# First stage of a hybrid diffusion step: roots of the token norms by pairs of tiles with a GpSimd power, and another order of weight loads and steps

## The chip, the cores and the metric

The kernel runs on one core of one Trainium2 chip. The metric is the device time of one execution in microseconds (us); the time before is the median of three runs. One further execution was taken with the hardware profiler, and every row and start time below is from it. The engines are called as in the profile: PE is TensorE (PEld its weight loads), DVE is VectorE, ACT is ScalarE, POOL is GpSimd, SP is SyncE, which here only issues DMAs.

## The reference, cut to what matters

One layer of a diffusion backbone works on 128 context tokens and 512 latent tokens, five tiles of 128 tokens, with 1024 channels, all in float32. The stage that is changed is the very first one:

```python
def rms_scale(x):
    xf = x.astype(jnp.float32)
    return xf * lax.rsqrt(jnp.mean(xf * xf, axis=-1, keepdims=True) + EPS)

def adaln(cond, w_mod, b_mod):
    m = jax.nn.silu(cond) @ w_mod + b_mod
    return jnp.split(m[..., None, :], 6, axis=-1)
...
        sh1, sc1, g1, sh2, sc2, g2 = adaln(c_ctx, w_mod[l], b_mod[l])
        h = rmsnorm(xp, norm1_g[l]) * (1.0 + sc1) + sh1
        y, (k_c, v_c, sf_c, sb_c) = token_mixer(h, *mix_w, pos_ctx, None)
```

`token_mixer` begins with `z = h @ w_in`. The kernel computes the columns of `z` for keys and values first, and those products end the stage. Attention, retention, the output projections and the gated MLP follow; none of their source is changed.

## The kernel before, in words

**Tiling.** The five token tiles lie in `xin`, tokens on the partitions. Each tile's sum of squares is taken on ACT (`x_square`, L340, with an accumulator that is read out after each tile), the reciprocal root on DVE (`rsqrt`, L202 to L220: an integer first guess and three Newton steps), and each tile is scaled in place on DVE (L349). PE transposes a scaled tile in eight 128x128 blocks, four to a PSUM bank (`x_trans`, L356), and the banks are copied out (L358) into `xnT`, two tiles `f0.s.1` and `f0.s.2` that hold channel blocks 0 to 3 and 4 to 7 with the channels on the partitions. PSUM has five banks for this (`mm1.mm`) and three more (`aux1.aux`).

**adaLN.** The product of the two condition vectors with the first 2048 columns of `w_mod` is cut into five groups (`MG`): groups 0 and 1 of one channel block each, groups 2, 3 and 4 of two. For group g, `mod_load(g)` loads the weights, `mod_mm(g)` is the product on PE (L368), `mod_row(g)` copies its result on DVE (L376), and `mod_vec(g)` turns the row into per-channel factors with one small matmul (L382) and two small DVE operations (L384, L386).

**Keys and values.** For each channel block k, `mod_hi(k)` applies the factors to `xnT` on DVE (L391, two instructions) and rounds the result into `hT[0]` on ACT (L393); `mod_lo(k)` forms the rest that rounding left in `hT[1]` on DVE (L396). The weights are split likewise, two channel blocks at a time: `kv_hi(k)` on ACT (L319), `kv_lo(k)` on DVE (L324). `z_kv(k)` then runs 15 matmuls of 128x512 on PE, three for each of five token tiles (`mm3`, L159 to L161): high times high, high activations times low weights (this one waits for `kv_lo`), low activations times high weights (this one waits for `mod_lo`). The five banks accumulate over k from 0 to 7. `z_kv(k, g)` with a second argument places `mod_vec(g)` behind its second token tile, so that PE still has nine matmuls after the small one.

**What sets the order.** Inside the block that begins at L406 the order of PE, DVE and ACT is the written one (`manual_schedule`). After the block, DVE and ACT go back to the scheduler, which also mixes in early work of the next stage. DMAs are issued by SP in the order in which they are written from L327 on; each waits for buffers, and for earlier DMAs on its semaphore. The weight buffers `raw` number two and the split ones (`wh`) eight, so the loads of the next stage wait until these splits are done. The next stage starts with the query columns (`a_group`, L175), whose first matmuls follow the last of `z_kv(7)` on PE. Of POOL the first stage makes no use: its first arithmetic is at L525, for the rotary tables. A similar power of -0.5 on POOL, with one Newton step behind it on DVE, stands at the end of the kernel (`root`, L1250 to L1258).

Of the kernel before, what the change touches and what calls it, by code (L numbers as in the profile page):

```python
# [69 lines left out]
def hybrid_step(ctx: ExitStack, tc: tile.TileContext, a: dict, o: dict):  # L70
# [265 lines left out]
    nc.sync.dma_start(cst[:, C_RF:], a["cst"][:, C_RF:])

# [2 lines left out]
        nc.scalar.activation(sq, xin[:, t, :], AF.Square, accum_out=ss[:, t:t + 1])  # L340

    def x_scale(t0, t1_, on_act=()):
        rs = rsqrt(t1, ss[:, t0:t1_], t1_ - t0, 1.0 / DM)
        for t in range(t0, t1_):
            r = rs[:, t - t0:t - t0 + 1]
            if t in on_act:
                nc.scalar.activation(xin[:, t, :], xin[:, t, :], AF.Copy, scale=r)
            else:
                V.tensor_scalar(xin[:, t, :], xin[:, t, :], r, None, op0=ALU.mult)  # L349

    def x_trans(t):
        for g in range(2):
            ps = mm([P, 512], tag="mm")
            for j in range(4):
                k = g * 4 + j
                nc.tensor.transpose(ps[:, j * P:(j + 1) * P], xin[:, t, k * P:(k + 1) * P], ident)  # L356
# [1 line left out]
            copy(xnT[g][:, :, t * P:(t + 1) * P], ps.rearrange("p (k t) -> p k t", k=4))  # L358
# [1180 lines left out]
```

## Time and profile before

| what | value |
| --- | --- |
| median of three runs | 1196.1 us (1194.02 to 1198.86) |
| the profiled execution: its own time | 1197.29 us |
| the profiled execution: its span, first to last instruction | 1195.5 us |
| instructions | 18334 |
| 0 to 15.5 us: PE busy, DVE busy, ACT busy | 0.37, 4.01, 7.25 us |
| 27.15 to 38.0 us: PE busy, mean granted clock | 10.85 us, 0.84 |
| 38.0 to 49.9 us: PE busy, mean granted clock | 11.77 us, 1.00 |
| 49.9 to 64.0 us: PE busy, mean granted clock | 14.10 us, 1.00 |
| 120 to 1107 us: PE busy | 983.5 of 987 us |

How to read it: the span is one microsecond or two shorter than the time, which includes what lies around the instructions. The rows by stretch of time are from the view of windows. PE's busy time counts each matmul to its modelled end, so that a PE that is shown busy can still have short waits between matmuls. The last `z_kv` matmul starts at 63.83 us, and the first of the query columns at 64.06 us.

### The profile page before, as it was taken

Reading aid. Unit: us, or ns where it says so; the run is one execution under the profiler, and the core shown is the slowest. Engines: PE = TensorE matmul, PEld = TensorE weight load, DVE = VectorE, ACT = ScalarE, POOL = GpSimd, SP = SyncE. Lnnn points to the kernel's source line nnn. Section 1 sums busy time; section 2 is a strip of 40 time slices with the busy share of each in tenths; the row PEclk is TensorE's granted clock in tenths of the full one; section 3 lists DMA queues with packets and bytes.
Section 4 is the critical chain, followed back from the end, with each engine's and each line's share of the span. In section 5 each row is a group of like instructions: output and inputs, shape, how many; then the busy total and the mean of one; then the engine's idle time right before and its main releaser. Section 6 shows DMA issues by size and latency. Waiting matters only on the chain. (4 is left out here: it accounts for less than half of the span.)

```text
span 1195.5 us, 18334 instructions
## 1 busy us (share of the span) xinstructions
PE 1155.4 (97%) x7317; PEld 1040.5 (87%) x7317; DVE 735.7 (62%) x1429; ACT 569.3 (48%) x1022; POOL 173.5 (15%) x176
## 2 busy tenths in 40 slices
PE   3999999999999999999999999999999999999994
PEld 3788899999988888888999988999999899899884
...
GB/s 283 280 108 71 36 36 36 36 57 166 201 210 154 141 98 44 36 36 71 36 77 89 169 124 183 76 106 124 130 126 174 153 91 147 125 134 168 122 140 88
DMA packets 131205, 140.07 MB, mean 117 GB/s; under 512 B 26272, under 2 KB 98032, under 8 KB 131120
## 3 DMA queue, kind: packets, MB, share of 16 engines
...
q14 instruction: 28, 0.23, 0.1%
...
## 5 line engine op out<-in xcount | busy, mean ns | idle before, releaser
L791 POOL TENSOR_TENSOR ret.r2k.6_3635<-ret.u5.5_3528,ret.u1.1_3521 128x256 f32<-128x256 f32 x2 | 1.4, 740 | 205.1 <-ACT ret.u5.5_3528 L787 205.1
L1353 DVE TENSOR_TENSOR t7.u4.4_6930<-t7.u4.4_6930,const.u1.1_70 128x322 f32<-128x322 f32 x10 | 4.9, 494 | 10.1 <-ACT const.u1.1_70 L1352 10.1
L840 DVE SCALAR_TENSOR_TENSOR ret2.u1.1_4322<-ret2.u1.1_4322,const.u14.14_94 64x128 f32<-64x128 f32 x24 | 6.8, 336 | 6.6 <-ACT ret2.u1.1_4322 L833 6.5
L525 POOL TENSOR_TENSOR p1.u1.1_618<-p1.u3.3_622,p1q.u1.1_612 128x512 f32<-128x512 f32 x1 | 1.6, 1567 | 58.6 <-DMA p1.u4.4_624<-in_cache_k 58.6
L152 DVE TENSOR_TENSOR weights.wh.183_6570<-weights.raw.181_6567,weights.wh.182_6569 128x1024 fp32r<-128x1024 f32 x1 | 1.2, 1224 | 14.3 <-ACT weights.wh.182_6569 L147 14.3
L356 PE MATMUL mm1.mm.1_180<-const.u1.1_70,xin.u1.1_112 128*128 128x128 f32 x4 | 1.1, 434 | 9.2 <-DVE xin.u1.1_112 L349 9.2
L1264 POOL TENSOR_TENSOR x1.u1.1_6381<-x1.u1.1_6381,weights.raw.410_10994 128x512 f32<-128x512 f32 x5 | 7.4, 1499 | 16.0 <-ACT x1.tm.112_11007 L1242 9.8
L842 DVE SCALAR_TENSOR_TENSOR ret2.u1.1_4322<-ret2.u1.1_4322,const.u14.14_94 64x128 f32<-64x128 f32 x24 | 6.6, 382 | 4.8 <-ACT ret2.u1.1_4322 L835 4.8
L793 DVE TENSOR_TENSOR ret.u5.5_3528<-ret.u5.5_3528,ret.u1.1_3521 128x512 f32<-128x512 f32 x5 | 3.5, 692 | 9.4 <-POOL ret.r2k.8_3706 L791 3.3
L393 ACT CAST acts.u1.1_100<-f0.s.1_113 128x640 fp32r<-128x640 f32 x4 | 2.9, 727 | 12.9 <-DVE f0.s.1_113 L391 12.9
L793 DVE TENSOR_TENSOR ret.u4.4_3527<-ret.u4.4_3527,ret.u1.1_3521 128x512 f32<-128x512 f32 x5 | 3.5, 692 | 9.0 <-POOL ret.r2k.11_3886 L791 4.7
L356 PEld LDWEIGHTS mm1.mm.1_180<-const.u1.1_70,xin.u1.1_112 128*128 128x128 f32 x4 | 0.7, 216 | 9.4 <-DVE xin.u1.1_112 L349 9.4
L393 ACT CAST acts.u1.1_100<-f0.s.2_114 128x640 fp32r<-128x640 f32 x4 | 2.9, 730 | 9.9 <-DVE f0.s.2_114 L391 9.9
L152 DVE TENSOR_TENSOR weights.wh.108_4352<-weights.raw.106_4349,weights.wh.107_4351 128x1024 fp32r<-128x1024 f32 x1 | 1.2, 1224 | 10.3 <-ACT weights.wh.107_4351 L147 10.3
L147 ACT CAST weights.wh.112_4507<-weights.raw.111_4505 128x1024 fp32r<-128x1024 f32 x1 | 1.0, 1049 | 13.3 <-PE mm3.mm.36_4220 L160 13.3
L902 POOL TENSOR_TENSOR f0.s.5_3525<-f0.s.5_3525,ret2.ny20.11_4904 128x512 f32<-128x512 f32 x5 | 6.0, 1236 | 9.1 <-DVE ret2.ny20.11_4904 L219 9.1
L494 ACT ACTIVATE f0.s.3_724<-f0.s.3_724,p1q.ny20.11_892 128x128 f32<-128x128 f32 x20 | 6.0, 388 | 2.5 <-DVE p1q.ny20.11_892 L217 2.5
...
L259 DVE COPY mod2.wr.9_4312<-aux3.aux.15_4279 128x128 f32<-128x128 f32 x1 | 0.3, 291 | 10.9 <-PE aux3.aux.15_4279 L256 10.9
L1236 DVE TENSOR_TENSOR x1.u1.1_6381<-x1.u1.1_6381,gate.u1.1_5311 128x512 f32<-128x512 f32 x10 | 6.9, 686 | 0.0
L147 ACT CAST weights.wh.67_3361<-weights.raw.66_3359 128x1024 fp32r<-128x1024 f32 x1 | 1.0, 1044 | 11.5 <-PE mm3.mm.8_3143 L195 11.5
L147 ACT CAST weights.wh.72_3539<-weights.raw.71_3537 128x1024 fp32r<-128x1024 f32 x1 | 1.0, 1044 | 11.5 <-PE mm3.mm.12_3298 L195 11.5
...
## 6 DMA issues: line engine op xcount, KB each, us to landing
...
xin.u1.1_112<-in_x_sample SPq DMA_DIRECT2D x4, 512.0 KB
p0.u5.5_130<-in_w_mod SPq DMA_DIRECT2D x2, 1024.0 KB
p0.u6.6_135<-in_w_mod SPq DMA_DIRECT2D x2, 1024.0 KB
p0.u7.7_138<-in_w_mod SPq DMA_DIRECT2D x2, 1024.0 KB
...
```

What stands on the lines that cost most here:

```text
L147: nc.scalar.copy(hi, rv)
L152: (lo_eng or V).tensor_sub(lo, rv, hi.bitcast(F32))
L356: nc.tensor.transpose(ps[:, j * P:(j + 1) * P], xin[:, t, k * P:(k + 1) * P], ident)
L393: nc.scalar.copy(hT[0][:, k, :], xk)
L494: nc.scalar.activation(x[:, j], x[:, j], AF.Copy, scale=rstd[:, j:j + 1])
L793: V.tensor_mul(z, z, r1[:, t, 0:1, :].to_broadcast([P, 8, 64]))
L840: V.scalar_tensor_tensor(Ss[0:64, hh, st + 1, j], Ss[0:64, hh, st, j], cdsel[0:64, h:h + 1], Ss[0:64, hh, st + 1, j], op0=ALU.mult, op1=AL ...
L842: V.scalar_tensor_tensor(Ss[64:128, hh, 2 - st, j], Ss[64:128, hh, 3 - st, j], cdsel[64:128, h:h + 1], Ss[64:128, hh, 2 - st, j], op0=ALU. ...
L902: nc.gpsimd.tensor_mul(ov, ov, rso[:, 4 * t:4 * t + 4].unsqueeze(2).to_broadcast([P, 4, P]))
L1236: V.tensor_mul(x1[:, t, gs], x1[:, t, gs], gb[:, t == 0, gs])
L1264: eng.tensor_mul(x, x, fg[:, c0:c0 + 512])
L1353: V.tensor_sub(u[1][:, hi_u], u[1][:, hi_u], u3[i])
```

## The change

The roots of the token norms are no longer taken for three tiles and then two, but for tiles 0 and 1, then 2 and 3, then 4. The integer first guess and two of the three Newton steps are gone; a power of -0.5 on POOL (`x_sum`) and one Newton step on DVE (`x_root`) stand in their place. `x_scale`, `x_trans` and the copy out of PSUM (`x_evac`) are separate calls now, so that they can be put in any order, and the first adaLN product `mod_mm(0)` stands between the transposes of tiles 2 and 3. The constant -0.5 for the power moves in the constants' table, so that it comes with the first of its two loads. In the DMA order `mod_load(2)` goes ahead of `kv_load(2, 2)`, and `mod_load(3)` ahead of `kv_load(4, 4)`. Behind `z_kv(0)` the steps stand in another order: `kv_hi(2)` and `kv_lo(2)`, which were ahead of `mod_mm(2)`, come after `mod_hi(2)`; `kv_hi(4)` and `kv_lo(4)` come after `mod_hi(4)`; and `mod_mm(4)` stands behind `z_kv(4)`, not ahead of it, so that `mod_vec(4)` is inside `z_kv(5)`.

```diff
-C_ID, C_SEL, C_SEL1, C_JV, C_RF, C_RB, C_MF, C_MB, C_IQ, C_NH, C_W = 0, 128, 136, 140, 142, 270, 398, 526, 654, 786, 787
+C_ID, C_SEL, C_SEL1, C_JV, C_NH, C_RF, C_RB, C_MF, C_MB, C_IQ, C_W = 0, 128, 136, 140, 142, 143, 271, 399, 527, 655, 787
...
     mod_load(1)
+    mod_load(2)
     kv_load(2, 2)
-    mod_load(2)
+    mod_load(3)
     kv_load(4, 4)
-    mod_load(3)
     mod_load(4)
...
-    def x_scale(t0, t1_, on_act=()):
-        rs = rsqrt(t1, ss[:, t0:t1_], t1_ - t0, 1.0 / DM)
...
+    def x_sum(t0, n):
+        m, mh, y = (t1([P, n], tag=f"{g}{t0}") for g in ("xm", "xh", "xy"))
+        V.tensor_scalar(m, ss[:, t0:t0 + n], 1.0 / DM, EPS, op0=ALU.mult, op1=ALU.add)
+        nc.gpsimd.tensor_tensor(y, m, cst[:, C_NH:C_NH + 1].to_broadcast([P, n]), op=ALU.pow)
+        V.tensor_scalar(mh, m, -0.5, None, op0=ALU.mult)
+        xr[t0] = mh, y
+
+    def x_root(t0, n):
+        mh, y = xr[t0]
+        tt = t1([P, n], tag=f"xt{t0}")
+        if n == 1:
+            V.scalar_tensor_tensor(tt, y, mh, y, op0=ALU.mult, op1=ALU.mult)
+        else:
+            V.tensor_mul(tt, y, y)
+            V.tensor_mul(tt, tt, mh)
+        V.scalar_tensor_tensor(y, tt, 1.5, y, op0=ALU.add, op1=ALU.mult)
...
-        x_scale(0, 3)
+        x_sum(0, 2)
+        x_root(0, 2)
+        x_scale(0)
         x_trans(0)
+        x_scale(1)
         x_trans(1)
+        x_sum(2, 2)
+        x_evac(0, 0, A)
+        x_evac(0, 1, A)
+        x_root(2, 2)
+        x_scale(2)
+        x_sum(4, 1)
+        x_evac(1, 0, A)
+        x_trans(2)
+        x_scale(3)
+        x_root(4, 1)
+        x_scale(4)
+        x_evac(1, 1, A)
+        mod_mm(0, False)
+        x_evac(2, 0, A)
+        x_trans(3)
+        x_evac(2, 1, D)
+        mod_row(0)
+        x_evac(3, 0, A)
+        x_evac(3, 1, D)
+        x_trans(4)
+        mod_vec(0)
+        x_evac(4, 0, A)
+        x_evac(4, 1, D)
         kv_hi(0)
-        x_scale(3, 5)
-        x_trans(2)
-        x_trans(3)
-        x_trans(4)
-        mod_mm(0)
-        mod_vec(0)
...
         z_kv(0)
-        kv_hi(2)
-        kv_lo(2)
         mod_mm(2)
         z_kv(1, 2)
         mod_hi(2)
+        kv_hi(2)
+        mod_lo(2)
+        kv_lo(2)
         mod_hi(3)
-        mod_lo(2)
         mod_lo(3)
         z_kv(2)
-        kv_hi(4)
-        kv_lo(4)
         mod_mm(3)
         z_kv(3, 3)
         mod_hi(4)
+        kv_hi(4)
+        mod_lo(4)
+        kv_lo(4)
         mod_hi(5)
-        mod_lo(4)
         mod_lo(5)
         kv_hi(6)
         kv_lo(6)
+        z_kv(4)
         mod_mm(4)
-        z_kv(4, 4)
+        z_kv(5, 4)
         mod_hi(6)
+        mod_lo(6)
         mod_hi(7)
-        mod_lo(6)
         mod_lo(7)
-        z_kv(5)
```

Three places show how the instructions stand now. The first is the start of the stage on DVE. Before, the root of three tiles (`ssx` holds the sums of squares) begins so:

```order
L207 TENSOR_SCALAR p0.nm3.10_160<-p0.ssx.2_115 128x3
L208 TENSOR_SCALAR p0.ni3.11_161<-p0.nm3.10_160 128x3
L209 TENSOR_SCALAR p0.ny3.12_162<-p0.ni3.11_161 128x3
L210 TENSOR_SCALAR p0.nm3.10_160<-p0.nm3.10_160 128x3
L215 TENSOR_TENSOR p0.nt3.13_163<-p0.ny3.12_162 128x3
L216 TENSOR_TENSOR p0.nt3.13_163<-p0.nt3.13_163,p0.nm3.10_160 128x3
L217 SCALAR_TENSOR_TENSOR p0.ny3.12_162<-p0.nt3.13_163,p0.ny3.12_162 128x3
```

The last three of these, one Newton step, follow twice more, and then L349 scales tiles 0, 1 and 2.

Of the change, on the same engine and at the same place (`xy0` and `xy2` come from POOL, which has one instruction of L347 for each pair):

```order
L346 TENSOR_SCALAR p0.xm0.10_160<-p0.ssx.2_115 128x2
L348 TENSOR_SCALAR p0.xh0.11_161<-p0.xm0.10_160 128x2
L357 TENSOR_TENSOR p0.xt0.13_166<-p0.xy0.12_162 128x2
L358 TENSOR_TENSOR p0.xt0.13_166<-p0.xt0.13_166,p0.xh0.11_161 128x2
L359 SCALAR_TENSOR_TENSOR p0.xy0.12_162<-p0.xt0.13_166,p0.xy0.12_162 128x2
L364 TENSOR_SCALAR xin.u1.1_112<-xin.u1.1_112,p0.xy0.12_162 128x1024 x2
```

Thirteen small operations before the first scale have become five, and they wait for two tiles' sums, not three; between L348 and L357 DVE waits for POOL.

The second place is ACT from the first channel block to `kv_hi(6)`. Before, with `weights.wh.5`, `wh.7` and `wh.9` the high parts of the key and value weights from k = 2, 4 and 6 on (the first row is blocks 0 and 1, the third blocks 2 and 3, the fifth blocks 4 and 5):

```order
L393 CAST acts.u1.1_100<-f0.s.1_113 128x640 x2
L319 CAST weights.wh.5_338<-weights.raw.1_124 128x1024
L393 CAST acts.u1.1_100<-f0.s.1_113 128x640 x2
L319 CAST weights.wh.7_419<-weights.raw.2_133 128x1024
L393 CAST acts.u1.1_100<-f0.s.2_114 128x640 x2
L319 CAST weights.wh.9_485<-weights.raw.2_133 128x1024
```

And in the changed kernel, where the cast of `mod_hi` is at L411:

```order
L411 CAST acts.u1.1_100<-f0.s.1_113 128x640 x3
L319 CAST weights.wh.5_390<-weights.raw.1_124 128x1024
L411 CAST acts.u1.1_100<-f0.s.1_113 128x640
L411 CAST acts.u1.1_100<-f0.s.2_114 128x640
L319 CAST weights.wh.7_471<-weights.raw.2_136 128x1024
L411 CAST acts.u1.1_100<-f0.s.2_114 128x640
L319 CAST weights.wh.9_480<-weights.raw.2_136 128x1024
```

The weight split for k = 2 stood ahead of the cast of block 2 and stands behind it now, and the one for k = 4 stands behind the cast of block 4.

The third place is DVE in the same stretch of the changed kernel, from the row of group 2 to block 3. Here L394 to L404 are `mod_row` and `mod_vec`, L409 and L414 are `mod_hi` and `mod_lo`, and L324 is `kv_lo(2)`, which stood ahead of all of these before:

```order
L394 COPY p0.mrow.24_366<-aux1.aux.6_333 128x128
L402 TENSOR_TENSOR p0.u1.1_111<-aux1.aux.7_374,const.u3.3_83 128x2x4
L404 TENSOR_TENSOR p0.u1.1_111<-p0.u1.1_111,const.u3.3_83 128x4
L409 TENSOR_SCALAR f0.s.1_113<-f0.s.1_113,p0.u1.1_111 128x512
L409 TENSOR_SCALAR f0.s.1_113<-f0.s.1_113,p0.u1.1_111 128x128
L414 TENSOR_TENSOR acts.u2.2_101<-f0.s.1_113,acts.u1.1_100 128x640
L324 TENSOR_TENSOR weights.wh.6_391<-weights.raw.1_124,weights.wh.5_390 128x1024
```

Block 3's own L409 and L414 follow behind this L324, where before both blocks' L391 came one after the other.

More of the change, by code (lines that the diff above doesn't have):

```diff
@@ L340, in x_square, with x_scale, x_evac @@
         nc.scalar.activation(sq, xin[:, t, :], AF.Square, accum_out=ss[:, t:t + 1])
-    def x_scale(t0, t1_, on_act=()):
-        rs = rsqrt(t1, ss[:, t0:t1_], t1_ - t0, 1.0 / DM)
[L344 to L349, printed above, removed]
+    xr = {}
+    def x_sum(t0, n):
[13 more added lines that the diff above has]
+        V.scalar_tensor_tensor(y, tt, 1.5, y, op0=ALU.add, op1=ALU.mult)
+        for t in range(t0, t0 + n):
+            xr[t] = mh, y, y[:, t - t0:t - t0 + 1]
+    def x_scale(t):
+        V.tensor_scalar(xin[:, t, :], xin[:, t, :], xr[t][2], None, op0=ALU.mult)
+    xps = {}
     def x_trans(t):
         for g in range(2):
-            ps = mm([P, 512], tag="mm")
+            xps[t, g] = mm([P, 512], tag="mm")
             for j in range(4):
                 k = g * 4 + j
-                nc.tensor.transpose(ps[:, j * P:(j + 1) * P], xin[:, t, k * P:(k + 1) * P], ident)
-            copy = V.tensor_copy if g and t > 1 else nc.scalar.copy
-            copy(xnT[g][:, :, t * P:(t + 1) * P], ps.rearrange("p (k t) -> p k t", k=4))
+                nc.tensor.transpose(xps[t, g][:, j * P:(j + 1) * P], xin[:, t, k * P:(k + 1) * P], ident)
+    def x_evac(t, g, copy):
+        copy(xnT[g][:, :, t * P:(t + 1) * P], xps[t, g].rearrange("p (k t) -> p k t", k=4))
     mrow, psm = {}, {}
@@ L416, in hybrid_step @@
         V.tensor_copy(s128[:, :, 0:2], s32)
+        A, D = nc.scalar.copy, V.tensor_copy
         for t in range(NT):
             x_square(t)
-        x_scale(0, 3)
+        x_sum(0, 2)
+        x_root(0, 2)
+        x_scale(0)
         x_trans(0)
+        x_scale(1)
         x_trans(1)
-        kv_hi(0)
-        x_scale(3, 5)
-        x_trans(2)
-        x_trans(3)
-        x_trans(4)
-        mod_mm(0)
-        mod_vec(0)
+        x_sum(2, 2)
[21 more added lines that the diff above has]
+        x_evac(4, 1, D)
+        kv_hi(0)
         mod_mm(1, False)
@@ L435, in hybrid_step @@
         mod_hi(1)
+        mod_lo(1)
         kv_lo(0, 1)
-        mod_lo(1)
         kvb = [mm([P, 512], tag="mm") for _ in range(NT)]
         z_kv(0)
-        kv_hi(2)
-        kv_lo(2)
         mod_mm(2)
```

## The prediction

> **What bounds the kernel now.** I read the page first, then the waits of PE, then the timeline of the first 65 us, then windows around the places where PE pauses.
>
> ```profile
> PE 1155.4 (97%) x7317; PEld 1040.5 (87%) x7317; DVE 735.7 (62%) x1429; ACT 569.3 (48%) x1022; POOL 173.5 (15%) x176
> PE mm1.mm.1_180 L356 <- DVE xin.u1.1_112 L349: 9.2, 1, 9.2
> 14.69 2.08 DVE L349 TENSOR_SCALAR xin.u1.1_112<-xin.u1.1_112,p0.ny3.12_162 128x1024 f32<-128x1024 f32 x3
> 15.50 1.11 PE L356 MATMUL mm1.mm.1_180<-const.u1.1_70,xin.u1.1_112 128*128 128x128 f32 x4 [9.15 <-DVE xin.u1.1_112 L349]
> 27.18 0.48 PE L159 MATMUL mm1.mm.11_318<-weights.wh.3_204,acts.u1.1_100 128*128 128x512 f32 x1
> ```
>
> PE is busy for 97% of the span, and its only long waits are in the first stage: 9.2 us for the first scaled tile, then the way to the first `z_kv` matmul at 27.18. From there to the query columns it hardly stops. So a gain here is a gain of the whole only if PE reaches the end of `z_kv(7)` sooner, and each new pause of PE behind 27.18 takes from it at full price.
>
> **The roots.** Before, the first scale waits for three sums and thirteen small operations.
>
> ```profile
> 10.82 0.19 ACT L340 ACTIVATION_READ_ACCUMULATOR acts.u2.2_101<-xin.u1.1_112 128x1 f32 x1
> 12.32 0.17 DVE L207 TENSOR_SCALAR p0.nm3.10_160<-p0.ssx.2_115 128x3 f32<-128x3 f32 x1 [4.82 <-ACT acts.u2.2_101 L340]
> 1174.78 0.17 DVE L1249 TENSOR_SCALAR t7.rm.28_11067<-t7.rm.28_11067 128x3 f32<-128x3 f32 x1
> 1175.95 0.17 DVE L1251 TENSOR_SCALAR t7.rm.28_11067<-t7.rm.28_11067 128x3 f32<-128x3 f32 x1 [1.00 <-POOL t7.ry.29_11068 L1250]
> 1189.78 0.54 POOL L1250 TENSOR_TENSOR t7.ry.35_11182<-t7.rm.34_11181,const.u1.1_70 128x1 f32<-128x1 f32 x1 [7.47 <-DVE t7.rm.34_11181 L1249]
> 59.00 1.57 POOL L525 TENSOR_TENSOR p1.u1.1_618<-p1.u3.3_622,p1q.u1.1_612 128x512 f32<-128x512 f32 x1 [58.55 <-DMA p1.u4.4_624<-in_cache_k]
> 62.38 1.30 POOL L525 TENSOR_TENSOR p1q.u2.2_613<-p1.u3.3_622,p1q.u1.1_612 128x512 f32<-128x512 f32 x1
> ```
>
> Two sums are there at 10.82 + 0.19 = 11.0. The same root stands at the end of the kernel: from L1249's start to DVE's next step it takes 1175.95 - 1174.78 = 1.17. Three small operations of 0.2 follow, so the first scale starts at 11.0 + 1.2 + 0.6 = 12.8 and not at 14.69: 1.9 sooner. POOL's part, for two columns, lies between the 0.54 that one column takes and 1.27: the 1.00 for which DVE waited with three columns, plus the 0.27 by which POOL's first tensor operation is longer than the same one later (1.57 against 1.30). So the gain is 1.6 to 2.3. The roots of tiles 2, 3 and 4 lie beside PE's first four banks of transposes, where 15.50 - 14.69 = 0.8 lies between scale and transpose as before.
>
> **The transposes and the first products.** PE starts at 13.6.
>
> ```profile
> 17.26 1.06 PE L356 MATMUL mm1.mm.3_192<-const.u1.1_70,xin.u1.1_112 128*128 128x128 f32 x4
> 20.86 0.60 PE L356 MATMUL mm1.mm.9_250<-const.u1.1_70,xin.u1.1_112 128*128 128x128 f32 x4
> 21.29 0.60 PE L356 MATMUL mm1.mm.10_256<-const.u1.1_70,xin.u1.1_112 128*128 128x128 f32 x4
> 21.82 1.08 PE L368 MATMUL aux1.aux.2_262<-p0.u3.3_121,p0.s128.8_146 128*32 128x128 f32 x32
> 23.32 0.39 PE L382 MATMUL aux1.aux.3_281<-const.u1.1_70,p0.mrow.18_279 128*128 128x4 f32 x2 [0.41 <-DVE p0.mrow.18_279 L376]
> 20.39 0.68 DVE L358 COPY f0.s.2_114<-mm1.mm.6_232 128x512 f32<-128x512 f32 x1
> ```
>
> The third bank starts 17.26 - 15.50 = 1.76 behind the first, 0.88 for each; those at the end take 21.29 - 20.86 = 0.43. Four slow ones, six fast ones and `mod_mm(0)` with 1.08 and some 0.2 at its edges make 3.5 + 2.6 + 1.3 = 7.4, so `mod_vec(0)` comes at 20.9 to 21.5 and not at 23.32. From it to `z_kv(0)` there are 27.18 - 23.32 = 3.9 before; now one copy of 0.68 out of PSUM stands in this chain on DVE. So `z_kv(0)` starts at about 25.7: **-1.5 us** (between -1.0 and -2.2). I take -1.5, since `mod_mm(1)` cannot go much ahead: its weights come with the transfers below.
>
> **The loads.** SP issues them in order, and the engines are full.
>
> ```profile
> 13.81 1.06 ACT L340 ACTIVATE acts.u2.2_101<-xin.u1.1_112 128x1024 fp32r<-128x1024 f32 x1 [0.24 <-DMA xin.u1.1_112<-in_x_sample]
> 21.80:27.10 5.30, 2.67 (x69) 2.09 (x68) 3.73 (x9) 1.01 (x2) 0.00 (x0) 1.00 1.09 355
> p0.u5.5_130<-in_w_mod SPq DMA_DIRECT2D x2, 1024.0 KB
> 32.40 1.95 PE L368 MATMUL aux1.aux.6_342<-p0.u5.5_130,p0.s128.8_146 128*32 128x128 f32 x64
> ```
>
> The last tile of x lands at 13.8, where ACT's wait ends. At 355 GB/s, five transfers of 128x1024 float32 (groups 0 and 1 and the first weights, 2.6 MB) take 7.4, to 21.2: `mod_mm(1)` has its weights just in time. Group 2 (two of 1024 KB) now comes next, at about 27, and `kv_load(2, 2)` at about 28.6. `mod_mm(2)` starts at 32.40 before, and now behind `z_kv(0)` at some 30.9: nothing of the new DMA order is waited for, and it saves nothing that PE waited for either, so it costs 0. Had `z_kv(0)` no pause at all, the wait would be under 0.5. The rotary tables' loads now stand behind one more weight load on SP. POOL waited for them until 59.0 (the L525 row); what it makes of them is for the keys, behind `z_kv(7)`, and the query columns' matmuls, which need none of it, cover a few us more. I count 0.
>
> **The new order behind `z_kv(1)`.** Here are the steps for k = 2 before:
>
> ```profile
> 29.22 1.04 ACT L319 CAST weights.wh.5_338<-weights.raw.1_124 128x1024 fp32r<-128x1024 f32 x1
> 30.30 1.23 DVE L324 TENSOR_TENSOR weights.wh.6_339<-weights.raw.1_124,weights.wh.5_338 128x1024 fp32r<-128x1024 f32 x1
> 35.78 0.28 PE L382 MATMUL aux1.aux.7_383<-const.u1.1_70,p0.mrow.20_375 128*128 128x8 f32 x2
> 36.50 1.52 DVE L391 TENSOR_SCALAR f0.s.1_113<-f0.s.1_113,p0.u1.1_111 128x512 f32<-128x512 f32 x4
> 37.34 1.44 ACT L393 CAST acts.u1.1_100<-f0.s.1_113 128x640 fp32r<-128x640 f32 x2 [7.07 <-DVE f0.s.1_113 L391]
> 37.85 0.40 PE L161 MATMUL mm1.mm.15_322<-weights.wh.3_204,acts.u2.2_101 128*128 128x512 f32 x1
> 38.12 0.50 PE L159 MATMUL mm1.mm.11_318<-weights.wh.5_338,acts.u1.1_100 128*128 128x512 f32 x1
> 38.46 0.40 PE L160 MATMUL mm1.mm.11_318<-weights.wh.6_339,acts.u1.1_100 128*128 128x512 f32 x1
> 38.98 0.50 PE L161 MATMUL mm1.mm.11_318<-weights.wh.5_338,acts.u2.2_101 128*128 128x512 f32 x1
> ```
>
> L319 and L324, 1.04 and 1.23, ran under `z_kv(0)`. Now L319 stands on ACT behind the cast of block 2, and L324 on DVE behind block 2's rest. Counted from L382: DVE starts L391 at +0.7 and has block 2 at +1.5, ACT casts it by +2.25, then the weights by +3.25 and DVE their rest by +4.55. PE has work until 37.85 + 0.23 = 38.08, that is +2.3 (matmuls follow each other every 0.23). The first matmul of `z_kv(2)` then waits 1.0, runs, and the second waits for L324 another 1.0: 2.1 in all. Before, these were 0.04 and, for the third matmul, 0.29. **+1.8 us.** What is queued behind on ACT and DVE is block 3, which PE needs only 3.5 later.
>
> For k = 4 the same chain starts at `mod_vec(3)`, with the same nine matmuls to cover it.
>
> ```profile
> 47.98 1.95 PE L368 MATMUL aux1.aux.10_489<-p0.u7.7_138,p0.s128.8_146 128*32 128x128 f32 x64
> 49.86 0.50 PE L159 MATMUL mm1.mm.11_318<-weights.wh.7_419,acts.u1.1_100 128*128 128x512 f32 x1
> 54.65 1.55 DVE L396 TENSOR_TENSOR acts.u2.2_101<-f0.s.2_114,acts.u1.1_100 128x640 fp32r<-128x640 f32 x2
> ```
>
> Before, `mod_mm(4)` with 1.95 lay here, and `z_kv(4)` began without a wait. Now it comes behind `z_kv(4)`, so its cover is gone, and the split of the weights is in the chain: **+2.1 us**. And `mod_vec(4)`, which had all of `z_kv(5)` ahead of its use, now has nine matmuls: the cast of block 6 is there at +2.3, its rest (L396, 0.8 for one block) at +3.15 from L382, so PE waits some 0.4 at the third matmul: **+0.4 us**. The bounds of these three are 0, if ACT and DVE keep ahead in a way that these rows don't show, and 4.9, if each hand-over costs 0.1 more. I take 4.3, as the durations are all rows of this trace.
>
> **The clock.** After a pause PE can run at half speed for a while.
>
> ```profile
> 21.86:25.27 3.41, 2.44 (x67) 1.89 (x66) 2.37 (x7) 0.40 (x2) 0.00 (x0) 1.00 1.08 359
> 25.27:28.69 3.42, 1.75 (x9) 1.50 (x10) 2.63 (x8) 0.65 (x2) 0.00 (x0) 1.00 1.10 351
> 28.69:32.10 3.41, 3.41 (x10) 2.58 (x8) 2.52 (x3) 1.57 (x2) 0.00 (x0) 0.50 1.05 377
> 134.50:137.91 3.41, 2.60 (x15) 1.75 (x14) 3.41 (x9) 2.26 (x9) 1.43 (x2) 1.00 0.00 0
> ```
>
> In windows (busy time of PE first, granted clock third from the end), 3.4 us with PE busy 1.75 are followed by 3.4 us at clock 0.50; 2.44 or 2.60 busy are not. Half speed for 3.4 us costs 1.7 of PE work. The pauses at k = 2 and k = 4 are 2.1 us within 2.3; a stretch of 3.4 us that holds nearly all of one has PE busy for about 1.3. Whether a stretch does hangs on where its edge falls: 2.3 plus some slack fits in 3.4 a little over half the time. So of the two pauses I count one: **+1.7 us** (0 to 3.4). The half-speed stretch in `z_kv(0)` is there before and stays, since PE pauses ahead of it as long as before.
>
> The Trainium skill, in TensorE: Matmul & The Clock Gate, Part 1, says that the slow clock comes after at least one idle window of about 3.4 us; by that alone pauses of 1 us would cost no clock, and the sum would be 1.7 lower. This trace does not agree with it at the letter: the stretch ahead of the slow one was busy for 1.75 of its 3.42 us.
>
> **Sum.** -1.5 + 1.8 + 2.1 + 0.4 + 1.7 = +4.5 us. The profiled execution took 1197.3, 1.2 above the median of 1196.1. From the median: 1196.1 + 4.5 = 1200.6. Behind the stage PE is bound as before, so the shift stays to the end. About 0.5%, 6 us, is what a measurement of this kernel can tell from no change.
>
> **Rivals.** (a) Both pauses fall into one window each: -1.5 + 4.3 + 3.4 = +6.2, 1202.3. For it: the pauses are alike; against it: the edge is free. (b) Neither does: +2.8, 1198.9. (c) The pauses don't appear, so only the gain is left: 1194.6. For it: ACT has room, with 1.57 of 3.41 us busy even from 28.69 on; against it: the order on ACT is fixed, and a cast behind another cannot start sooner. (d) POOL is not ready for the first power. This decides for slower.
>
> ```profile
> L525 POOLq EVENT_SEMAPHORE  x3: 17/43/38291, 20.5 to 59.2; - x3
> L525 POOLq MODIFY_POOL_CONFIG  x2: 11/11/11, 0.7 to 0.8; - x2
> ```
>
> POOL's queue configures itself at 0.7 to 0.8, and the next record is a wait that begins at 20.5. Before, nothing asks POOL for anything in between. If it is busy until 20.5 with what the configuration started, the power that I put at 11.3 starts 9.2 later, and the time is 1200.6 + 9.2 = 1209.8; it decides from the point where POOL is ready later than some 13.2, when the 1.9 of the root is used up. Against it: a wait's record may begin when its first condition is met, not when POOL comes free.
>
> The Trainium skill, in GPSIMD Engine Reference, section 2.1, gives about 6 us for the load behind such a configuration; by it POOL is ready at 6.8 as an estimate, and (d) costs nothing. The rows here only bound the load between 0 and 19.7 us.
>
> **How the numbers follow.** Forecast with one slow window 0.45; (a) 0.22; (b) 0.15; (c) 0.12; (d) 0.06. The predicted time is 1200.6. The range reaches from (c) to over (a): 1194.0 to 1204.0; with it only (d) and the tails are left out. Slower by over 6 us, that is over 1202.1: half of (a), a tenth of the forecast and (d), 0.22. Faster, under 1190.1: 0.02. The rest, 0.76, is within 0.5%.
>
> **What the profile will show.** Right: the first L364 near 12.8, the first transpose near 13.6, `z_kv(0)` near 25.7; PE waiting for ACT (L319) and then for DVE (L324) at `z_kv(2)` and again at `z_kv(4)`, about 1 us each; a clock of 0.50 behind at least one of them; the last `z_kv` matmul near 68 and not 63.83. Wrong: no such waits, a first scale behind 20, or a wait for `in_w_mod`. What would make the prediction wrong most easily is the clock, which each execution draws anew.

## The result, and the profile after

Over twenty runs of each kernel, the kernel before has a median of 1196.81 us (1193.76 to 1199.74) and the changed one 1201.16 us (1198.15 to 1203.0): a ratio of 1.0029, with a 95% interval of 1.002 to 1.0039. By the medians the change makes the kernel slower by 4.4 us, by the ratio by 3.5. That is less than the 0.5% that the prediction set as its bound, but the interval does not hold 1, so the change does make the kernel slower. The profiled execution of the changed kernel took 1202.09 us, 4.8 above the one of before.

The start of the changed kernel, from the timeline (start, duration, engine, line, what is written and read, and in brackets how long the engine was idle and for whom it waited):

```profile
10.69 0.19 ACT L340 ACTIVATION_READ_ACCUMULATOR acts.u2.2_101<-xin.u1.1_112 128x1 f32 x1
10.91 0.17 DVE L346 TENSOR_SCALAR p0.xm0.10_160<-p0.ssx.2_115 128x2 f32<-128x2 f32 x1 [3.48 <-ACT acts.u2.2_101 L340]
11.16 0.70 POOL L347 TENSOR_TENSOR p0.xy0.12_162<-p0.xm0.10_160,const.u1.1_70 128x2 f32<-128x2 f32 x1 [10.71 <-DVE p0.xm0.10_160 L346]
12.48 1.42 DVE L364 TENSOR_SCALAR xin.u1.1_112<-xin.u1.1_112,p0.xy0.12_162 128x1024 f32<-128x1024 f32 x2
13.29 0.47 PE L373 MATMUL mm1.mm.1_171<-const.u1.1_70,xin.u1.1_112 128*128 128x128 f32 x1 [7.03 <-DVE xin.u1.1_112 L364]
22.92 1.07 PE L386 MATMUL aux1.aux.4_280<-p0.u4.4_126,p0.s128.8_146 128*32 128x128 f32 x28 [0.69 <-DMA p0.u4.4_126<-in_w_mod]
25.76 0.69 PE L159 MATMUL mm1.mm.11_313<-weights.wh.3_277,acts.u1.1_100 128*128 128x512 f32 x1
```

POOL starts its power at once when DVE has the mean, and takes 0.70 us for two columns. The first scale starts at 12.48, not at 14.69, and PE at 13.29, 2.2 us sooner than before. Of that, 1.42 us reach the first `z_kv` matmul (25.76 against 27.18). On the way six banks of transposes run slow (13.29 to 17.61, 0.86 each) and not four, and `mod_mm(1)` waits 0.69 for its weights. That wait costs nothing by itself: it and the wait for the row copy behind it (1.53) make 2.22, as long as the row copy alone was waited for before, and in the profile of e5 below, where PE doesn't wait for the weights, it waits 2.2 for the row copy.

What is lost comes behind it. These are PE's waits in the changed kernel from 20 to 75 us (waiting line, for whom, us in total, times, longest):

```profile
PE aux1.aux.5_304 L400 <- DVE p0.mrow.23_302 L394: 1.5, 1, 1.5
PE mm1.mm.11_313 L159 <- ACT weights.wh.5_390 L319: 0.8, 1, 0.8
PE mm1.mm.11_313 L159 <- ACT weights.wh.7_471 L319: 0.8, 1, 0.8
PE mm1.mm.11_313 L160 <- DVE weights.wh.8_472 L324: 0.8, 1, 0.8
PE mm1.mm.11_313 L160 <- DVE weights.wh.6_391 L324: 0.8, 1, 0.8
PE aux1.aux.4_280 L386 <- DMA p0.u4.4_126<-in_w_mod: 0.7, 1, 0.7
PE mm1.mm.11_313 L161 <- DVE acts.u2.2_101 L414: 0.2, 1, 0.2
```

The four for L319 and L324 are not in the list of the kernel before. The chain that makes the pause at `z_kv(2)`, and the last `z_kv` matmul, in the timeline:

```profile
35.92 0.73 ACT L411 CAST acts.u1.1_100<-f0.s.1_113 128x640 fp32r<-128x640 f32 x1 [8.03 <-DVE f0.s.1_113 L409]
36.55 1.04 ACT L319 CAST weights.wh.5_390<-weights.raw.1_124 128x1024 fp32r<-128x1024 f32 x1
37.63 1.23 DVE L324 TENSOR_TENSOR weights.wh.6_391<-weights.raw.1_124,weights.wh.5_390 128x1024 fp32r<-128x1024 f32 x1
37.65 0.49 PE L159 MATMUL mm1.mm.11_313<-weights.wh.5_390,acts.u1.1_100 128*128 128x512 f32 x1 [0.81 <-ACT weights.wh.5_390 L319]
38.91 0.50 PE L160 MATMUL mm1.mm.11_313<-weights.wh.6_391,acts.u1.1_100 128*128 128x512 f32 x1 [0.77 <-DVE weights.wh.6_391 L324]
...
69.89 0.40 PE L161 MATMUL mm1.mm.15_317<-weights.wh.9_480,acts.u2.2_101 128*128 128x512 f32 x1
```

ACT casts the block, then the weights; DVE forms their rest; and PE waits for each in turn: 0.81, then 0.77. Between starts that follow each other the pauses are 0.98 and 1.03 above the usual 0.23. At `z_kv(4)` the same two waits stand at 50.59 and 51.85. The stage ends at 69.89, not at 63.83, so it lost 6.06 from end to end, or 7.48 from the first `z_kv` matmul on. Waits don't make that alone; the view of windows (busy time of each engine with PE first, granted clock third from the end) shows the rest:

```profile
22.48:25.89 3.41, 1.44 (x31) 1.18 (x32) 2.73 (x6) 1.14 (x2) 0.00 (x0) 0.99 1.09 348
25.89:29.30 3.41, 3.41 (x10) 2.63 (x10) 2.50 (x6) 0.72 (x1) 0.00 (x0) 0.50 1.08 362
36.07:39.48 3.41, 1.83 (x8) 0.95 (x7) 2.68 (x4) 1.52 (x2) 0.00 (x0) 1.00 1.07 365
39.48:42.89 3.41, 3.41 (x10) 2.67 (x9) 0.91 (x2) 0.72 (x1) 0.00 (x0) 0.50 1.09 348
49.72:53.13 3.41, 1.83 (x8) 1.25 (x8) 2.68 (x4) 1.40 (x2) 0.00 (x0) 1.00 0.00 0
53.13:56.55 3.42, 3.42 (x10) 2.58 (x8) 3.12 (x4) 2.99 (x4) 0.00 (x0) 0.50 0.01 1
```

Three stretches of 3.4 us run at half clock, the first in `z_kv(0)` as before, one behind each new pause. Two more than before cost 2 x 1.7 = 3.4. With the pauses of 2.0 and 2.0, less 0.3 that the third matmul of `z_kv(2)` waited before, and 0.34 at `z_kv(6)`, this makes 7.5.

The stage lost more than the whole. The first matmul of the query columns starts 6.2 us later than before (70.26 against 64.06), and so does the matmul that stood at 1083.65 (now 1089.90); but the one at 1125.26 is only 4.8 later. Between them the execution of before ran one stretch at half clock, and that of the changed kernel none:

```profile
1107.29:1110.70 3.41, 1.23 (x6) 0.70 (x5) 0.89 (x1) 0.80 (x1) 0.00 (x0) 1.00 0.97 236
1110.70:1114.12 3.42, 3.42 (x9) 2.65 (x8) 2.07 (x3) 1.23 (x2) 0.00 (x0) 0.50 1.05 358
```

PE waits 2.2 us for the same weights just ahead of this place in both profiles. So the same wait can be followed by half clock in one execution and not in another, and 1.4 us of the difference between the two profiled times are chance.

### The profile page after: what moved, and what is told of

It is laid out like the page before. It is cut to its first block, busy times and chain, and to the rows that moved or that the text cites. A ratio compares the mean times of both kernels' runs of the same rounds, so it can differ in the third digit from the quotient of the medians.

```text
span 1200.3 us, 18331 instructions
## 1 busy us (share of the span) xinstructions
PE 1159.9 (97%) x7317; PEld 1042.4 (87%) x7317; DVE 735.0 (61%) x1417; ACT 569.8 (47%) x1022; POOL 175.8 (15%) x179
## 4 chain that ended last, share of the span: by engine, by line
PE 84%; DVE 8%; ACT 3%; issue 2%; DMA 2%; POOL 1%; SPq 0%; POOLq 0%; ACTq 0%; DVEq 0%
DMA weights.raw.383_10440<-in_w_up 1%; POOL f0.s.5_3520 L941 0%; DMA weights.raw.402_10788<-in_w_down 0%; DVE acts.u2.2_101 L1105 0%; DMA xin.u1.1_112<-in_x_sample 0%; DVE x1.u1.1_6376 L1264 0%; DVE x1.u1.1_6376 L1077 0%; DVE acts.u1.1_100 L1104 0%; DVE x1.u1.1_6376 L1276 0%; DVE x1.u1.1_6376 L1275 0%; DVE x1.u1.1_6376 L1271 0%; POOL x1.u1.1_6376 L1303 0%; PE mm7.mm.9_7496 L1381 0%; PE mm7.mm.45_9650 L1378 0%; PE mm7.mm.33_8918 L1378 0%
## 5 line engine op out<-in xcount | busy, mean ns | idle before, releaser
L152 DVE TENSOR_TENSOR weights.wh.183_6565<-weights.raw.181_6562,weights.wh.182_6564 128x1024 fp32r<-128x1024 f32 x1 | 1.2, 1224 | 14.3 <-ACT weights.wh.182_6564 L147 14.3
L411 ACT CAST acts.u1.1_100<-f0.s.2_114 128x640 fp32r<-128x640 f32 x4 | 2.9, 728 | 13.6 <-DVE f0.s.2_114 L409 13.6
L411 ACT CAST acts.u1.1_100<-f0.s.1_113 128x640 fp32r<-128x640 f32 x4 | 2.9, 726 | 13.6 <-DVE f0.s.1_113 L409 13.6
L152 DVE TENSOR_TENSOR weights.wh.108_4347<-weights.raw.106_4344,weights.wh.107_4346 128x1024 fp32r<-128x1024 f32 x1 | 1.2, 1225 | 10.3 <-ACT weights.wh.107_4346 L147 10.3
L147 ACT CAST weights.wh.112_4502<-weights.raw.111_4500 128x1024 fp32r<-128x1024 f32 x1 | 1.1, 1050 | 13.3 <-PE mm3.mm.36_4215 L160 13.3
L340 ACT ACTIVATE acts.u2.2_101<-xin.u1.1_112 128x1024 fp32r<-128x1024 f32 x5 | 5.3, 1057 | 3.0 <-DMA xin.u1.1_112<-in_x_sample 1.5
L147 ACT CAST weights.wh.182_6564<-weights.raw.181_6562 128x1024 fp32r<-128x1024 f32 x1 | 1.1, 1055 | 11.5 <-PE mm3.mm.83_6396 L160 11.5
```

Of the source, the lines that this page charges most:

```text
L147: nc.scalar.copy(hi, rv)
L152: (lo_eng or V).tensor_sub(lo, rv, hi.bitcast(F32))
L411: nc.scalar.copy(hT[0][:, k, :], xk)
```

## The experiments

Ten kernels were run, e2 and e6 five times, the others eleven or twelve times, each beside the kernel before on the same chip (e9 and e10 on another chip than the rest). The differences below are from the median of before in those rounds (1196.72 for e1 to e4, 1196.61 for e5 to e8, 1196.38 for e9 and e10). Where two kernels are compared, both are counted from before; the changed kernel stands at +4.4 in this. Two kernels whose intervals overlap are not told apart by their medians alone.

| kernel | median, us | from before, us | ratio, 95% interval |
| --- | --- | --- | --- |
| e1: the new start alone | 1195.08 | -1.6 | 0.998 (0.9971 to 0.9989) |
| e2: new loads and steps alone | 1203.85 | +7.1 | 1.0054 (1.0042 to 1.0067) |
| e3: changed kernel, splits put back | 1199.74 | +3.0 | 1.0022 (1.0012 to 1.0032) |
| e4: changed kernel, pauses filled | 1198.96 | +2.2 | 1.0017 (1.0008 to 1.0026) |
| e5: new start and new loads | 1194.51 | -2.1 | 0.9979 (0.997 to 0.9988) |
| e6: changed kernel, `mod_mm(4)` put back | 1202.69 | +6.1 | 1.0047 (1.0034 to 1.0061) |
| e7: e1, pause ahead of `z_kv(0)` filled | 1195.08 | -1.5 | 0.9984 (0.9975 to 0.9994) |
| e8: before, the same pause filled | 1195.74 | -0.9 | 0.9988 (0.9979 to 0.9997) |
| e9: e5, the same pause filled | 1193.52 | -2.9 | 0.9976 (0.9965 to 0.9987) |
| e10: e5, only `mod_mm(4)` moved | 1199.58 | +3.2 | 1.0023 (1.0014 to 1.0033) |

### The change in two halves: e1 and e2

e1 takes the new start and puts the DMA order and all steps behind `z_kv(0)` back. e2 is the reverse: the kernel before with

```diff
     mod_load(1)
+    mod_load(2)
     kv_load(2, 2)
-    mod_load(2)
+    mod_load(3)
     kv_load(4, 4)
-    mod_load(3)
```

and the changed order of steps from `z_kv(0)` on.

> Only the start of the change (roots by pairs with the POOL power, new order of scales, transposes, copies and mod_mm(0), and mod_lo(1) ahead of the second half of kv_lo(0)); loads and the steps behind z_kv(0) are as before. Theory (the start gains, the moved weight splits lose it): first z_kv matmul near 25.7 instead of 27.2, no pause at z_kv(2) or z_kv(4), last z_kv matmul near 62.3 instead of 63.83, time 1.5 us under before. Rival (the power on POOL and the start cost the time): 4 us over before.

> Only the new DMA order and the new order of steps behind z_kv(0); the start is as before. Theory: z_kv(0) at 27.2, pauses of 0.8 before the first and 0.8 before the second matmul of z_kv(2) and of z_kv(4), one or two stretches at clock 0.50 behind them, last z_kv matmul at 68 to 71.5, time 6 us over before (4.3 to 7.7). Rival (the start costs): same as before.

Measured: -1.6 and +7.1. In the trace of e1 PE makes no pause at `z_kv(2)` or `z_kv(4)`; in that of e2 the four waits for L319 and L324 of 0.8 each are there, and `z_kv` ends at 71.21. So the start gains what was expected, the rest of the change loses, and the halves add up to 5.5 against 4.4 measured for both together; the interval of e2 alone is 3 us wide. One expectation was missed: in the profile of e1 the last `z_kv` matmul stands at 63.19, not near 62.3, since this execution ran two stretches of `z_kv(0)` at half clock (24.56 to 31.39), one more than before.

### The clock: e4

e4 is the changed kernel with three matmuls more ahead of the first and three ahead of the second matmul of `z_kv(2)` and `z_kv(4)`, into a bank of PSUM that nothing reads. They run while PE would wait.

```diff
+        fb = aux([P, 512], tag="aux") if fill else None
+        for _ in range(fill):
+            nc.tensor.matmul(fb, hT[0][:, 0, :P], wkv[k - 2][1][:, :512], start=True, stop=True)
...
+            for _ in range(fill if t == 0 else 0):
+                nc.tensor.matmul(fb, hT[0][:, 0, :P], wkv[k - 2][1][:, :512], start=True, stop=True)
...
-        z_kv(2)
+        z_kv(2, None, 3)
...
-        z_kv(4)
+        z_kv(4, None, 3)
```

> The changed kernel with six matmuls more at z_kv(2) and six at z_kv(4), three ahead of the first matmul and three ahead of the second, into a PSUM bank that nothing reads: they keep PE busy for 0.7 us of each wait and add nothing to the result. Theory (a pause costs its own length and, by the half clock behind it, 1.7 us more): the waits for the splits end when they did, but the clock stays at 1.00 behind z_kv(2) and z_kv(4): last z_kv matmul near 66.6, time about 2.8 us over before, that is 1.5 to 2 us under the changed kernel's median. Rival (the clock is not set by these pauses): half clock behind them as before, time as the changed kernel's, 4.4 over before.

Measured: +2.2, that is 2.1 us under the changed kernel. The intervals of the two ratios overlap, but the slowest of e4's eleven runs took 1199.92, and twelve of the twenty runs of the changed kernel took longer. The mean granted clock, which is on record for every run, was 0.992 to 0.994 in e4 and 0.989 to 0.994 in the changed kernel. The last `z_kv` matmul stands at 66.70, near the 66.6 that was expected, and not at 69.89. The windows over the pause at `z_kv(2)`:

```profile
36.00:39.40 3.40, 3.22 (x13) 2.01 (x12) 2.67 (x4) 1.53 (x2) 0.00 (x0) 1.00 1.07 364
39.40:42.80 3.40, 3.40 (x33) 2.60 (x35) 0.93 (x2) 0.73 (x1) 0.00 (x0) 1.00 1.09 348
```

The useful matmuls still pause for 0.97 and 1.03 us, since the splits are as late as in the changed kernel. But PE is busy for 3.22 of 3.40 us, not 1.83, and the next stretch keeps the clock of 1.00; at `z_kv(4)` it is the same. So the half clock is a second cost of the pauses, about 2 us in the median, and it goes when PE no longer stands idle in them.

### Undoing one part: e3 and e6

e3 puts both splits back ahead of the adaLN products, and leaves the loads and `mod_mm(4)` where the change has them:

```diff
         z_kv(0)
+        kv_hi(2)
+        kv_lo(2)
         mod_mm(2)
         z_kv(1, 2)
         mod_hi(2)
-        kv_hi(2)
         mod_lo(2)
-        kv_lo(2)
...
+        kv_hi(4)
+        kv_lo(4)
         mod_mm(3)
...
-        kv_hi(4)
         mod_lo(4)
-        kv_lo(4)
```

> The changed kernel with one thing undone: kv_hi(2), kv_lo(2) stand ahead of mod_mm(2) again, and kv_hi(4), kv_lo(4) ahead of mod_mm(3); the new DMA order, the new start and mod_mm(4) behind z_kv(4) stay. Theory: both pauses and the slow clock behind them are gone, what stays is -1.5 for the start and +0.4 at z_kv(6): 1.1 us under before, last z_kv matmul near 62.8. Rival (the DMA order makes the pauses, the weights of k = 2 and 4 land too late): PE waits at z_kv(2) and z_kv(4) as in the changed kernel, 3 to 4 us over before.

This was a miss: 1199.74, 3.0 over before, not 1.1 under it. The pauses went, as meant, but others came, in the list of PE's waits of e3:

```profile
PE mm1.mm.11_313 L159 <- ACT acts.u1.1_100 L411: 1.5, 1, 1.5
PE aux1.aux.6_337 L386 <- DMA p0.u5.5_129<-in_w_mod: 0.7, 1, 0.7
PE mm1.mm.11_313 L161 <- DVE acts.u2.2_101 L414: 0.6, 1, 0.6
PE aux1.aux.7_378 L400 <- DVE p0.mrow.24_370 L394: 0.4, 1, 0.4
```

`mod_mm(2)` waits for its weights, and behind it for its row copy: this execution ran all of `z_kv(0)` at full clock (1.00 from 18 to 31.2 us), without any fill, so that `mod_mm(2)` came 2.7 us sooner than in the changed kernel. `z_kv(6)` waits for both halves of its block (1.5 and 0.6). At this point either the loads or the place of `mod_mm(4)` could have made the waits at `z_kv(6)`.

e6 undoes the other part, the place of `mod_mm(4)`:

```diff
-        z_kv(4)
         mod_mm(4)
-        z_kv(5, 4)
+        z_kv(4, 4)
+        z_kv(5)
```

> The changed kernel with only the product mod_mm(4) put back ahead of z_kv(4), its vector work back inside z_kv(4), and z_kv(5) behind it without them. Theory: in the changed kernel the move costs only the wait of z_kv(6) that its profile shows, 0.2 us in a gap of 0.3, since the two pauses ahead of it leave the vector engine time; the time goes from 1201.2 to between 1200.4 and 1201.2. Rival: put back, the product ahead of z_kv(4) fills part of the pause there (2.0 us of product beside a split that was the last to come): the waits of z_kv(4) for its weights shrink or go, and the time falls by up to 2 us, to 1199.2.

Neither came true: the time was 1202.69, 1.7 us over the changed kernel and not under it. These are five runs, though, and the intervals of the two ratios overlap. The timeline of e6:

```profile
49.05 1.96 PE L386 MATMUL aux1.aux.10_484<-p0.u7.7_138,p0.s128.8_146 128*32 128x128 f32 x64
49.91 1.23 DVE L324 TENSOR_TENSOR weights.wh.8_472<-weights.raw.2_136,weights.wh.7_471 128x1024 fp32r<-128x1024 f32 x1
51.05 0.80 DVE L409 TENSOR_SCALAR f0.s.2_114<-f0.s.2_114,p0.u1.1_111 128x512 f32<-128x512 f32 x2
52.64 0.83 DVE L414 TENSOR_TENSOR acts.u2.2_101<-f0.s.2_114,acts.u1.1_100 128x640 fp32r<-128x640 f32 x1 [0.79 <-ACT acts.u1.1_100 L411]
53.59 1.23 DVE L324 TENSOR_TENSOR weights.wh.10_481<-weights.raw.2_136,weights.wh.9_480 128x1024 fp32r<-128x1024 f32 x1
54.73 0.28 DVE L394 COPY p0.mrow.26_517<-aux1.aux.10_484 128x128 f32<-128x128 f32 x1
55.07 0.39 PE L400 MATMUL aux1.aux.11_525<-const.u1.1_70,p0.mrow.26_517 128*128 128x8 f32 x2 [2.44 <-DVE p0.mrow.26_517 L394]
```

The product does cover the late split: `z_kv(4)` no longer waits. But its row copy (L394) stands on DVE behind two splits, the scale of block 5 and the rest of block 5, and comes 3.7 us after the product. PE stops for it 2.44 us inside `z_kv(4)`. One pause is traded for another: with three stretches at half clock in the stage, as in the changed kernel, the first matmul of the query columns starts at 70.48, after a wait of 0.87 for a copy on DVE (L553), against 70.26 there. The profiled execution of e6 is 1.4 us longer because it ran a stretch at half clock near 1117 as well. So what is shown is that putting `mod_mm(4)` back alone brings nothing where the splits are late; that it costs 1.7 is not shown.

### Loads and `mod_mm(4)` apart: e5 and e10

e5 is e1 with the new DMA order and nothing else. e10 is e5 with only this:

```diff
-        mod_mm(4)
-        z_kv(4, 4)
+        z_kv(4)
+        mod_mm(4)
+        z_kv(5, 4)
...
-        z_kv(5)
         z_kv(6)
```

> The new start with the new order of loads, and every step behind z_kv(0) as before. Against e1_start_only it differs in the order of the loads alone, against e3_splits_back in the place of mod_mm(4) (with the vector work of its group) and in the order of the mod_lo steps. Theory 1, the third group's adaLN product moved into z_kv(5) is what stopped z_kv(6) in e3_splits_back (waits of 1.5 and 0.6 us there): that pause is gone here, z_kv(6) follows with gaps below 0.3 us, and the time is 2.1 us under that run's 1199.7, near 1197.6. Theory 2, the new load order is what delays: the waits of mod_mm(2) for its weights (0.7) and of the row product behind it (0.4) stay in both theories if the order of loads makes them, so 1.1 us over e1_start_only's 1195.1, near 1196.2. Rival: the order of loads costs nothing, as the prediction had it: 1195.1, within 0.5.

> e5_start_and_loads with only mod_mm(4) moved behind z_kv(4) and its vector work into z_kv(5), as in the change. Against e3_splits_back only the order of the mod_lo steps differs. Theory: this move is the whole loss of e3_splits_back, z_kv(6) waits about 2.1 us for its halves again, and the time is 1194.5 + 2.1 to 1199.7, that is 1196.6 or more. Rival: the order of the mod_lo steps made the loss, z_kv(6) follows without a wait and the time is 1194.5 within 0.6.

e5 took 1194.51, 2.1 under before. From 20 to 75 us the list of PE's waits has one line:

```profile
PE aux1.aux.5_304 L400 <- DVE p0.mrow.23_302 L394: 2.2, 1, 2.2
```

There is no pause at `z_kv(6)` and no wait for `in_w_mod`. Theory 2 fell, so the loads were not what delayed e3, and the rival (1195.1 within 0.5) was nearest. Theory 1 had the cause right and its price too low: 1197.6 counted only the waits. e10 took 1199.58, 5.3 over e5 and level with e3, so the order of the `mod_lo` steps made no difference that these runs show. What the move does stands in e10's timeline (L152 and L147 split weights of the next stage, which the scheduler mixes in):

```profile
54.45 0.28 PE L400 MATMUL aux1.aux.11_540<-const.u1.1_70,p0.mrow.26_532 128*128 128x8 f32 x2
54.77 0.17 DVE L402 TENSOR_TENSOR p0.u1.1_111<-aux1.aux.11_540,const.u3.3_83 128x8 f32<-128x8 f32 x1 [0.26 <-PE aux1.aux.11_540 L400]
54.85 1.21 DVE L152 TENSOR_TENSOR weights.wh.15_732<-weights.raw.11_725,weights.wh.14_731 128x1024 fp32r<-128x1024 f32 x1
55.98 0.16 DVE L404 TENSOR_TENSOR p0.u1.1_111<-p0.u1.1_111,const.u3.3_83 128x4 f32<-128x4 f32 x1
56.17 1.52 DVE L409 TENSOR_SCALAR f0.s.2_114<-f0.s.2_114,p0.u1.1_111 128x512 f32<-128x512 f32 x4
56.72 1.05 ACT L147 CAST weights.wh.17_797<-weights.raw.16_795 128x1024 fp32r<-128x1024 f32 x1 [5.75 <-PE mm1.mm.15_317 L160]
57.67 1.35 ACT L411 CAST acts.u1.1_100<-f0.s.2_114 128x640 fp32r<-128x640 f32 x2
58.44 0.50 PE L159 MATMUL mm1.mm.11_313<-weights.wh.9_480,acts.u1.1_100 128*128 128x512 f32 x1 [1.52 <-ACT acts.u1.1_100 L411]
```

With `mod_vec(4)` inside `z_kv(5)`, its chain L402, L404, L409, L411 has nine matmuls of PE to hide behind. Here two early splits have slipped into that chain: L152 puts L404 1.21 behind L402, and L147 holds L411 until 1.50 after L409 starts. In the changed kernel's timeline the same chain is free:

```profile
60.56 0.17 DVE L402 TENSOR_TENSOR p0.u1.1_111<-aux1.aux.11_540,const.u3.3_83 128x8 f32<-128x8 f32 x1 [0.85 <-PE aux1.aux.11_540 L400]
60.80 0.12 DVE L404 TENSOR_TENSOR p0.u1.1_111<-p0.u1.1_111,const.u3.3_83 128x4 f32<-128x4 f32 x1
61.01 0.80 DVE L409 TENSOR_SCALAR f0.s.2_114<-f0.s.2_114,p0.u1.1_111 128x512 f32<-128x512 f32 x2
61.85 0.73 ACT L411 CAST acts.u1.1_100<-f0.s.2_114 128x640 fp32r<-128x640 f32 x1 [2.35 <-DVE f0.s.2_114 L409]
```

L404 is 0.24 behind L402 and L411 0.84 behind L409; the split that stands in e10's chain ran here at 56.61, ahead of the chain, and PE waits only 0.17 at `z_kv(6)`. The two differences, 0.97 and 0.66, make 1.6, about the 1.52 for which PE waits in e10. That the loss comes from where the scheduler put those splits is read from the rows; no kernel was run that keeps them out of e10's chain. Two more waits of e10 are not in e5's list: the second at `z_kv(6)` (0.6), and 0.7 at the first query matmul, which waits for a copy on DVE. The three make 2.8 of the 5.3. The profiled execution of e10 also ran one stretch more of `z_kv(0)` at half clock than that of e5; that is chance, and explains the two profiled times but not the two medians. What makes the rest of the 5.3 stays open.

### The pause ahead of `z_kv(0)`: e7, e8 and e9

All three add the same lines, eight unread matmuls where PE waits for the row copy of `mod_mm(1)`: e7 to e1, e8 to the kernel before, e9 to e5.

```diff
         mod_mm(1, False)
+        fb = aux([P, 512], tag="aux")
+        for _ in range(8):
+            nc.tensor.matmul(fb, wkv[0][1][:, :P], wkv[0][1][:, :512], start=True, stop=True)
```

> e1_start_only with eight matmuls more of 128x512, whose result nothing reads, between mod_mm(1) and the row product behind it, where TensorE waits 1.8 us for the vector engine. Theory: z_kv(0) ran at half clock there because of that wait (two stretches in the profile of e1_start_only); eight matmuls of about 0.23 us fill it, z_kv(0) runs at full clock, and the median falls from 1195.1 to about 1193.8, where the fastest runs of e1_start_only lie. Rival 1: the half clock has another cause, nothing changes, 1195.1. Rival 2: with z_kv(0) shorter, mod_mm(2) waits for its weights instead, and half or more of the gain is given back: 1194.5 to 1195.1, with a wait for the load in the list of waits.

> The kernel before with the same eight matmuls behind mod_mm(1), where TensorE waited 2.2 us. Theory: the half-clock stretch in z_kv(0) (28.7 to 32.1 us in the profile of before), 1.7 us longer than at full clock, goes, and the median of 1196.7 falls to about 1195.0. Rival: the stretch is paid elsewhere or stays, 1196.7.

> e5_start_and_loads with the eight unread matmuls between mod_mm(1) and its row product. In e7_start_fill, with the old order of loads, z_kv(0) ran at full clock and mod_mm(2) then waited for its weights, 1.5 us. Theory: the new order of loads brings them sooner, so that the wait shrinks to the 0.7 us of e3_splits_back or less, and the time is 1194.5 less about 1.0, near 1193.5. Rival: the load is as late here, the wait is 1.5 us as in e7_start_fill, and the time stays at 1194.5 to 1195.1: then the half clock in z_kv(0) costs nothing in either order.

In all three profiles the half clock in `z_kv(0)` is gone (e3's shows that chance can do this too, so the times must bear it out). e7 gained nothing from it, as its rival 2 had it. e8 gained 0.9 in the median, half of what was expected; but none of its eleven runs took over 1196.4, where nine of the 26 runs of before took 1197.7 or more, and its mean is 1.7 lower. e9 is at 1193.52, as expected. Why e7 and e9 differ stands in their timelines. e7, with the old DMA order:

```profile
23.05 2.12 PE L471 MATMUL aux1.aux.5_297<-weights.wh.3_277 128*128 128x512 f32 x8
25.15 0.48 PE L159 MATMUL mm1.mm.11_322<-weights.wh.3_277,acts.u1.1_100 128*128 128x512 f32 x1
30.71 1.94 PE L386 MATMUL aux1.aux.7_346<-p0.u5.5_130,p0.s128.8_146 128*32 128x128 f32 x60 [1.49 <-DMA p0.u5.5_130<-in_w_mod]
```

And e9, with the new one:

```profile
25.03 0.48 PE L159 MATMUL mm1.mm.11_322<-weights.wh.3_277,acts.u1.1_100 128*128 128x512 f32 x1
28.70 2.50 PE L386 MATMUL aux1.aux.7_346<-p0.u5.5_129,p0.s128.8_146 128*32 128x128 f32 x64
29.25 1.67 PEld L386 LDWEIGHTS aux1.aux.7_346<-p0.u5.5_129,p0.s128.8_146 128*32 128x32 f32 x60 [0.41 <-DMA p0.u5.5_129<-in_w_mod]
```

With the old order the weights of group 2 are there at 30.71, with the new one at 29.25. So the new DMA order brings a gain where `z_kv(0)` runs at full clock (e9 against e7: 1.3 to 1.6 us by the medians, though the intervals overlap, and 0.9 at the first query matmul of the two profiles, 61.52 against 62.38), and little where it does not (e5 against e1: 0.5 to 0.6, with intervals that overlap). e9 is the fastest of the kernels, 2.9 us under before; its interval overlaps that of e5.

## Why the prediction was right

The forecast was +4.5 us, and +4.4 was measured (+3.5 by the ratio). Its terms, one by one:

| term of the sum | predicted | found |
| --- | --- | --- |
| start: first scale, first `z_kv` matmul | 12.8, -1.5 | 12.48, -1.42; alone -1.6 (e1) |
| pause at `z_kv(2)` | +1.8 | 0.98 + 1.03 - 0.29 = +1.7 |
| pause at `z_kv(4)` | +2.1 | 0.98 + 1.03 = +2.0 |
| third matmul of `z_kv(6)` | +0.4 | 0.34 above the usual step |
| clock | +1.7 (one stretch) | +3.4 in the profiled execution; about 2.1 in the median (e4) |
| new DMA order | 0 | 0 to -0.6 as PE stood (e5 against e1); -0.9 to -1.6 once `z_kv(0)` is fast (e9 against e7) |

**The start.** The root on POOL was priced from the same root at the kernel's end and lay within its bounds: 0.70 us for two columns, between 0.54 and 1.27. Rival (d), a POOL that is not ready, is out: its first power begins at 11.16, 0.25 after L346 starts. That the first `z_kv` matmul came within 0.1 of the forecast is in part luck: PE started 0.3 sooner than forecast, the way to `mod_vec(0)` (L400, at 21.60) took 8.3 us and not 7.4, with six slow banks where the text counted four, and the rest of the way 4.2 and not 4.6.

**The pauses.** The order written for ACT and DVE gave the chain L409, L411, L319, L324, and both the places and the lengths were as worked out. Rival (c) is out. One thing that the text named as a sign of being wrong did appear, a wait for `in_w_mod`: not for group 2, but for group 1, whose weights the text had in place at 21.2 and PE had at 22.92. It cost nothing, as said above.

**The clock.** Forecast, rival (a) and rival (b) were three draws of one thing. The profiled execution drew (a). Of the twenty runs seven lie within 1198.1 to 1198.6, three within 1199.8 to 1200.9, and ten within 1201.5 to 1203.0, steps of about 1.7 to 2, as none, one and two stretches would give. The mean granted clock of each run goes with it: 0.993 or 0.994 for the seven, 0.991 or 0.992 for six of the ten, 0.989 for the four slowest. Which stretches a run drew remains an interpretation, since a single run has no trace and the clock counts those in `z_kv(0)` and near 1110 us too. By it the forecast's case of exactly one was the rarest, and its time fits because the median falls near the middle: that the sum hit to 0.1 is luck. The Trainium skill, in TensorE: Matmul & The Clock Gate, Part 1, has the slow clock after at least one idle window. Here it came after windows in which PE was busy for 1.83 of 3.41 us, and filling those windows kept the clock.

**What the working had wrong.** "So it costs 0" for the DMA order holds only for a PE that is late anyway; the wait that the text put under 0.5 for a `z_kv(0)` without a pause is 0.41 in e9 and 0.69 in e3. That the half clock in `z_kv(0)` "stays" was no certainty either: the profiles show none (e3), one and two stretches there. And the text treated the parts as a sum: "its cover is gone" puts a loss on `mod_mm(4)` that the changed kernel doesn't have, as e6 shows. By the medians, undoing the splits alone gains 1.3 (e3, +3.0 against the changed kernel's +4.4), undoing `mod_mm(4)` alone gains nothing (e6, +6.1), and undoing both gains 6.5 (e5). The first two differ from the changed kernel by less than their intervals can tell; the third is clear of it, and so is the 5.3 of e10 against e5. The pauses came out right since the whole new order was followed through at once; a price for each part by itself would have been wrong.
